# Attention over pairs of heads: scores, turned probabilities and values follow 1, 3 and 1 pieces of product behind each other in place of 3, 3 and 2

## The chip, the cores and the metric

The kernel runs on one NeuronCore of a Trainium2 chip. The metric is the device time of one execution in microseconds (us); of three executions of the kernel before, the median is 2475.26 us (2474.47 to 2476.66). Engines are named as in the profile: PE is the matrix engine (PEld its weight loads), DVE the vector engine, ACT the scalar engine, POOL the GpSimd engine, SP the engine whose queue issues the weight transfers.

## The reference, cut to what matters

The program is a two-layer decoder trunk over 256 rows of width 2048: a retention layer with its MLP, then a latent-attention layer with its MLP. The change touches only the attention of the second layer, with 16 heads, 128 + 64 query columns a head, 128 value columns a head:

```python
c_q = rms_norm(h @ w_dq, q_norm)
q = (c_q @ w_uq).reshape(b, s, H, MLA_NOPE_DIM + MLA_ROPE_DIM)
q_nope = rms_norm(q[..., :MLA_NOPE_DIM], q_nope_norm)
q_pe = apply_rope(rms_norm(q[..., MLA_NOPE_DIM:], q_pe_norm), cos[:, :, None], sin[:, :, None])
...
    sc = jnp.einsum('bhqd,bkhd->bhqk', qn, k_nope) + jnp.einsum('bhqr,bkr->bhqk', qp, k_pe)
    sc = sc.astype(jnp.float32) * scale
    sc = jnp.where(kpos[None, :] <= qpos[:, None], sc, -jnp.inf)
    p = jax.nn.softmax(sc, axis=-1).astype(v.dtype)
    return jnp.einsum('bhqk,bkhd->bqhd', p, v)
...
return o @ w_o
```

## The kernel before

Everything large is a product of weights with activations held on chip. Weights come in chunks ("pieces"): one SP transfer, then for each of two halves an ACT cast to a high part `wh` and a DVE subtraction to a low part `wl` (`split`, L185 and L186; pools of 5 each), then matmuls high x high, high x low, low x high (L246 to L248). A piece of the query product `uq` is 24 matmuls of 384 columns, one of the output product `wo` is 24 matmuls of 512 columns. In the attention stage the pieces are `uq0.0` to `uq7.2` (eight pairs of heads, three pieces a pair), then `wo`: pieces 0, 1, 2 of column block 0, the same of block 1, then the last piece of block 0 and of block 1, then blocks 2 and 3.

The order of all work beside the pieces is written out by a small queue. `later(n, fn)` files `fn` for `n` pieces from now; every piece ends with `tick()`, which raises the count of pieces by one and runs all that is due, in order of due number; `need(items, n)` runs the queue ahead of its due numbers, first due first, until a list has `n` entries. What a function of the queue emits stands in the source order of each engine at that point. The tile framework hands out buffers, sets the semaphores, and can place a ready instruction ahead of an earlier one that isn't ready, so the order of an engine in a trace differs in places from that of the source.

A pair of heads `b` passes through five functions:

- `query(b)`, run at the end of the pair's third piece: ACT scales the product into `qs` and squares it into `qu` (L981, L983), DVE sums (L984, L985) and makes `qn_m` (L174), POOL raises it to -1/2 (`qn_r`, L175), DVE multiplies `qs` by it (L992), rotates the last 64 columns (L850 to L853) and splits them into `qpp` (L1001, L1002). In the prediction this DVE work from L992 to L1002 is called the rotation.
- its `turn`: PE turns `qs` and `qpp` (`qntp`, `qptp`, L205), ACT copies them out of PSUM into `qt` (L1008) and `qpe` (L1013) and casts `qt` to its high part (L185), DVE makes the low part of `qt` (L186).
- `score(b)`: 20 matmuls into `s` (L1028 to L1033), which read both parts of `qt` and `qpe`; DVE masks into `p` (L1038) and takes the maximum `mx` (L1043); ACT the exponential (L1048); DVE the reciprocal (L1049); ACT the scaling (L1054).
- its `turn`: PE turns `p` into two PSUM tiles `ptp` (L1061), ACT copies each to `pt` (L1063).
- `values(b)`: PE multiplies into `ao` (L1072, L1073), ACT and DVE split it into `ot` (L185, L186), which is appended to `o_act`.

`qntp`, `qptp`, `ptp` and `ao` share two PSUM banks (tag `tp`). `qs`, `qu`, `qpp`, `qt`, `qpe`, `p` and `pt` share a pool of 14 buffers (`f2k`). A piece `g` of `wo` calls `need(o_act, 2g + 2)`, so the third piece wants six pairs done and the last pieces all eight.

With pieces counted from the start of `uq`, the due numbers before are: `query(b)` at 3b+3, its turn at 3b+6, `score` at 3b+9, the turn of `p` at 3b+12, `values` at 3b+14. At count 24 `wo` begins; at count 26 it needs six entries and `values(5)`, due at 29, is run ahead together with turn 7, score 6 and the turn of p 5; at count 30 it needs eight, and `values(6)`, the turn of p 7 and `values(7)` are run ahead one behind another. `x_tiles` also files four loads of residual blocks (`x_wo`, POOL's queue, L140) in this stretch.

Of the kernel before, what the change touches and what calls it, by code (L numbers as in the profile page):

```python
# [68 lines left out]
def yoco(ctx: ExitStack, tc: tile.TileContext, a):  # L69
# [4 lines left out]
    def f2k(shape, name, dtype=F32):  # L74
        return pool.tile([P, *shape], dtype, tag="f2k", bufs=14, name=name)

    def small(w, name):
        return pool.tile([P, w], F32, tag="small", bufs=36, name=name)
# [5 lines left out]
    def bank(tag, shape, name):  # L84
        t = psum.tile([P, 512], F32, tag=tag, bufs=4 if tag == "acc" else 2, name=name)
        return shaped(t, shape)

    def two_banks(name):
        return psum.tile([P, 2, 512], F32, tag="at", bufs=1, name=name)

    def act_tile(name, dtype=F32R):

        return pool.tile([P, 2, 2, S], dtype, tag="act", bufs=24, name=name)
# [5 lines left out]
    def later(n, fn):  # L99
        queue.append((clock[0] + n, next(count), fn))  # L100
# [67 lines left out]
    def rstds(total, sizes, name):  # L168

        w = total.free_size()  # L170
        m, r = small(w, f"{name}_m"), small(w, f"{name}_r")
        view = m.rearrange("p (t i h) -> p t i h", t=NT, i=len(sizes))
        for i, n in enumerate(sizes):
            nc.vector.tensor_scalar(view[:, :, i], total[:, :, i], 1.0 / n, EPS, op0=ALU.mult, op1=ALU.add)  # L174
        nc.gpsimd.tensor_tensor(r, m, neg_half[:, :w], op=ALU.pow)  # L175
        return r.rearrange("p (t i h) -> p t i h", t=NT, i=len(sizes))
# [5 lines left out]
    def split(h, l, src, scale=None):  # L182

        if scale is None:
            nc.scalar.copy(h, src)  # L185
            nc.vector.tensor_tensor(l, src, h.bitcast(F32), op=ALU.subtract)  # L186
        else:
            nc.scalar.activation(h, src, AF.Copy, scale=scale)
            nc.vector.scalar_tensor_tensor(
                l, src, scale, h.bitcast(F32), op0=ALU.mult, op1=ALU.subtract  # L190
            )
# [8 lines left out]
    def transposed(srcs, name):  # L200

        tp = bank("tp", [2, S], name)
        for j in range(2):
            for t in range(NT):
                nc.tensor.transpose(tp[:, j, t * P : (t + 1) * P], srcs(t, j), ident)  # L205
        return tp
# [637 lines left out]
    def pe_rope(dst, u, src, t, i, heads):  # L844


        def tab(j, lo, n):
            return pe_tabs[t][i][:, j, lo : lo + n].unsqueeze(1).to_broadcast([P, heads, n])

        nc.vector.tensor_tensor(dst, src, tab(0, 0, 64), op=ALU.mult)  # L850
        nc.vector.tensor_tensor(u[:, :, 0:32], src[:, :, 32:64], tab(1, 0, 32), op=ALU.mult)
        nc.vector.tensor_tensor(u[:, :, 32:64], src[:, :, 0:32], tab(1, 32, 32), op=ALU.mult)
        nc.vector.tensor_tensor(dst, dst, u, op=ALU.add)  # L853
# [122 lines left out]
    def query(acc, b):  # L976
        qr, qu = [], []
        sq = small(4 * NT, f"sq{b}").rearrange("p (t i h) -> p t i h", t=NT, i=2)
        for t in range(NT):
            q = f2k([2, 192], f"qs{b}{t}")  # L980
            nc.scalar.activation(q.rearrange("p h c -> p (h c)"), acc[t], AF.Copy, scale=rq[t])  # L981
            u = f2k([2, 192], f"qu{b}{t}")
            nc.scalar.activation(u.rearrange("p h c -> p (h c)"), acc[t], AF.Square, scale=rq[t])  # L983
            nc.vector.reduce_sum(sq[:, t, 0], u[:, :, 0:NOPE], axis=AX.X)  # L984
            nc.vector.reduce_sum(sq[:, t, 1], u[:, :, NOPE:], axis=AX.X)  # L985
            qu.append((q, u))
        r = rstds(sq, [NOPE, ROPE], f"qn{b}")
        for t in range(NT):
            q, u = qu[t]
            for i, cols in enumerate((slice(0, NOPE), slice(NOPE, NOPE + ROPE))):  # L990
                n = cols.stop - cols.start
                nc.vector.tensor_tensor(  # L992
                    q[:, :, cols], q[:, :, cols], r[:, t, i].unsqueeze(2).to_broadcast([P, 2, n]), op=ALU.mult
                )
            flat = u.rearrange("p h c -> p (h c)")
            pe = flat[:, 0 : 2 * ROPE]
            tmp = flat[:, 2 * ROPE : 4 * ROPE].rearrange("p (h c) -> p h c", h=2)
            pe_rope(pe.rearrange("p (h c) -> p h c", h=2), tmp, q[:, :, NOPE:], t, 1, 2)
            parts = f2k([2, 2, ROPE], f"qpp{b}{t}", F32R)
            pe = pe.rearrange("p (h c) -> p h c", h=2)  # L1000
            nc.vector.tensor_copy(parts[:, :, 0], pe)  # L1001
            nc.vector.tensor_tensor(parts[:, :, 1], pe, parts[:, :, 0].bitcast(F32), op=ALU.subtract)  # L1002
            qr.append((q, parts.bitcast(F32)))

        def turn():
            tp = transposed(lambda t, j: qr[t][0][:, j, 0:NOPE], f"qntp{b}")
            raw = f2k([2, S], f"qt{b}")
            nc.scalar.activation(raw, tp, AF.Copy, scale=gqn)  # L1008
            qt = [f2k([2, S], f"qt{b}{i}", F32R) for i in range(2)]
            split(qt[0], qt[1], raw)  # L1010
            tp = transposed(lambda t, j: qr[t][1][:, j].rearrange("p i c -> p (i c)"), f"qptp{b}")
            qpe = f2k([2, S], f"qpe{b}", F32R)
            nc.scalar.copy(qpe, tp)  # L1013
            later(3, lambda: score(b, qt, qpe))

        later(3, turn)

    def score(b, qt, qpe):

        sc = two_banks(f"s{b}")  # L1020
        for hh in range(2):
            for t in range(NT):
                dst = sc[:, hh, t * P : t * P + (t + 1) * P]
                qs = slice(t * P, (t + 1) * P)
                n = (t + 1) * P
                qh, ql = (i[:, hh, qs] for i in qt)
                kh, kl = (k_t[b][:, i, hh, :n] for i in range(2))
                nc.tensor.matmul(dst, qh, kh, start=True, stop=False)  # L1028
                nc.tensor.matmul(dst, qh, kl, start=False, stop=False)
                nc.tensor.matmul(dst, ql, kh, start=False, stop=False)  # L1030

                for i in range(2):
                    nc.tensor.matmul(dst, qpe[:, hh, qs], kpe_t[:, i, :n], start=False, stop=i == 1)  # L1033
        p = [f2k([2, (t + 1) * P], f"p{b}{t}") for t in range(NT)]
        for t in range(NT):
            cols = slice(t * P, t * P + (t + 1) * P)
            cut = mask[:, cols].unsqueeze(1).to_broadcast([P, 2, (t + 1) * P])
            nc.vector.tensor_tensor(p[t], sc[:, :, cols], cut, op=ALU.add)  # L1038
        neg = small(4, f"mx{b}")
        den = small(4, f"den{b}")  # L1040
        inv = small(4, f"inv{b}")
        for t in range(NT):
            nc.vector.tensor_reduce(neg[:, 2 * t : 2 * t + 2], p[t], axis=AX.X, op=ALU.max, negate=True)  # L1043
        for t in range(NT):
            for hh in range(2):
                i = 2 * t + hh
                view = p[t][:, hh]
                nc.scalar.activation(view, view, AF.Exp, bias=neg[:, i : i + 1], accum_out=den[:, i : i + 1])  # L1048
        nc.vector.reciprocal(inv, den)  # L1049
        for t in range(NT):  # L1050
            for hh in range(2):
                i = 2 * t + hh
                view = p[t][:, hh]
                nc.scalar.activation(view, view, AF.Copy, scale=inv[:, i : i + 1])  # L1054

        def turn():
            pt = []
            for hh in range(2):
                tp = bank("tp", [3 * P], f"ptp{b}{hh}")
                for i, src in enumerate((p[0][:, hh], p[1][:, hh, 0:P], p[1][:, hh, P:])):  # L1060
                    nc.tensor.transpose(tp[:, i * P : (i + 1) * P], src, ident)  # L1061
                o = f2k([3 * P], f"pt{b}{hh}")
                nc.scalar.copy(o, tp)  # L1063
                pt.append(o)
            later(2, lambda: values(b, pt))

        later(3, turn)

    def values(b, pt):
        o = bank("tp", [2, S], f"ao{b}")  # L1070
        for hh in range(2):
            nc.tensor.matmul(o[:, hh], v_s[b][:, 0, hh], pt[hh][:, 0:S], start=True, stop=False)  # L1072
            nc.tensor.matmul(o[:, hh, P:S], v_s[b][:, 1, hh], pt[hh][:, S:], start=False, stop=True)  # L1073
        v = act_tile(f"ot{b}")
        split_act(v, o)
        o_act.append(v)
# [109 lines left out]
```

## Time and profile before

| what | value |
|---|---|
| median of 3 runs | 2475.26 us |
| the profiled execution, its own time | 2474.51 us |
| its span | 2472.7 us |
| PE / PEld / DVE / ACT / POOL busy, share of the span | 99% / 83% / 88% / 65% / 10% |
| HBM traffic over the span | 210 GB/s |
| first and last turn of a query pair (`qntp` on PE) | 1578.2 us, 1697.1 us |
| first and last product of `ot` (`wo` on PE) | 1683.9 us, 1788.9 us |

The profile shows one execution; times in a trace are microseconds from the start of its span. A row of a timeline gives start, duration, engine, source line, operation, output and inputs by the program's names, and in brackets how long the engine had been idle and what released it. In the list of waits a row gives who waited for whom, the total, the number of waits and the longest. A window's row gives each engine's busy time in a stretch, the granted clock of PE (1.00 is full speed) and the DMA share. PE's matmuls are pipelined, so the start of the next one, not its own duration, tells what a matmul costs.

### The profile page before, as it was taken

How to read it: one execution, taken by the hardware profiler on the slowest of the kernel's cores; microseconds unless marked ns; L12 is line 12 of the kernel's file. 1: busy time of each engine (PE TensorE's matmuls, PEld its weight loads, DVE VectorE, ACT ScalarE, POOL GpSimd, SP SyncE). 2: the span in 40 equal slices, each digit the busy share in tenths (PEclk: the TensorE clock that was granted, in tenths of full speed). 3: DMA queues.
4: the chain of work that ended last, by engine and by line, in shares of the span. 5: the costliest groups of instructions: out<-in, count | busy, mean ns of one | idle time of the engine just before them, and what ended most of it. 6: DMA issues, size and time to landing. Idle time of an engine off the chain costs nothing.

```text
span 2472.7 us, 31711 instructions
## 1 busy us (share of the span) xinstructions
PE 2455.6 (99%) x11635; PEld 2060.0 (83%) x11635; DVE 2167.4 (88%) x2805; ACT 1606.1 (65%) x2253; POOL 251.6 (10%) x310
## 2 busy tenths in 40 slices
PE   9999999999999999999999999999999999999999
PEld 7888888888888888888888888998888888888887
DVE  7799899889899999999999967776689999999996
ACT  6566656556676667667666766676566666676663
POOL 7300011000010010110110101110000201101100
PEclk9999999999999999999999999999999999999999
DMA  9555567555564685684785564445545856857854
GB/s 328 211 174 205 196 205 234 199 192 201 198 236 182 209 262 216 213 254 172 246 263 196 192 228 168 153 155 179 199 174 199 261 212 209 268 203 225 266 192 153
DMA packets 93403, 521.04 MB, mean 211 GB/s; under 512 B 11072, under 2 KB 12224, under 8 KB 40000
## 3 DMA queue, kind: packets, MB, share of 16 engines
q1 hardware_dynamic: 71856, 472.83, 53.8%
q0 software_dynamic: 21248, 46.15, 8.5%
q8 instruction: 91, 1.49, 0.2%
q14 instruction: 64, 0.52, 0.1%
q10 hardware_dynamic: 144, 0.05, 0.0%
HBM read 479.14 MB, written 39.85 MB: 210 GB/s over the span
## 4 chain that ended last, share of the span: by engine, by line
PE 91%; DVE 4%; ACT 3%; issue 1%; POOL 1%; DMA 0%; SPq 0%; ACTq 0%; POOLq 0%; DVEq 0%
PE u_c L358 7%; PE u_c L356 7%; PE u_c L357 7%; PE d_c L357 6%; PE d_c L358 6%; PE d_c L356 6%; PE rk_acc L274 2%; PE rq_acc L274 2%; PE rp_c L356 2%; PE rp_c L357 2%; PE rp_c L358 2%; PE u_p L358 2%; PE u_p L356 2%; PE u_p L357 2%; PE d_p L356 2%; PE d_p L358 2%
## 5 line engine op out<-in xcount | busy, mean ns | idle before, releaser
L185 ACT CAST u_wh<-u_raw 128x1024 fp32r<-128x1024 f32 x362 | 347.9, 991 | 207.8 <-DVE u_raw L321 100.8
L185 ACT CAST d_wh<-d_raw 128x1024 fp32r<-128x1024 f32 x358 | 344.1, 993 | 202.5 <-DVE d_raw L321 93.9
L186 DVE TENSOR_TENSOR u_wl<-u_raw,u_wh 128x1024 fp32r<-128x1024 f32 x362 | 402.0, 1144 | 47.2 <-ACT u_wh L185 41.7
L186 DVE TENSOR_TENSOR d_wl<-d_raw,d_wh 128x1024 fp32r<-128x1024 f32 x358 | 397.8, 1146 | 40.1 <-ACT d_wh L185 35.5
L356 PE MATMUL u_c<-u_wh,n 128*128 128x512 f32 x706 | 276.4, 392 | 0.0
L357 PE MATMUL u_c<-u_wl,n 128*128 128x512 f32 x706 | 275.5, 390 | 0.0
L358 PE MATMUL u_c<-u_wh,n 128*128 128x512 f32 x706 | 274.9, 389 | 0.0
L356 PE MATMUL d_c<-d_wh,hid 128*128 128x512 f32 x654 | 256.0, 392 | 0.0
L357 PE MATMUL d_c<-d_wl,hid 128*128 128x512 f32 x654 | 255.4, 391 | 0.0
L358 PE MATMUL d_c<-d_wh,hid 128*128 128x512 f32 x654 | 254.6, 389 | 0.0
L185 ACT CAST rp_wh<-rp_raw 128x1024 fp32r<-128x1024 f32 (+1 forms) x166 | 160.7, 982 | 140.9 <-DVE rp_raw L321 64.9
L186 DVE TENSOR_TENSOR rp_wl<-rp_raw,rp_wh 128x1024 fp32r<-128x1024 f32 (+1 forms) x166 | 184.9, 1137 | 26.7 <-ACT rp_wh L185 24.4
L358 PEld LDWEIGHTS u_c<-u_wh,n 128*128 128x128 f32 x706 | 132.6, 188 | 27.4
L356 PEld LDWEIGHTS u_c<-u_wh,n 128*128 128x128 f32 x706 | 132.6, 188 | 26.9
L357 PEld LDWEIGHTS u_c<-u_wl,n 128*128 128x128 f32 x706 | 132.6, 188 | 26.7
L358 PEld LDWEIGHTS d_c<-d_wh,hid 128*128 128x128 f32 x654 | 122.8, 188 | 25.4
L356 PEld LDWEIGHTS d_c<-d_wh,hid 128*128 128x128 f32 x654 | 122.8, 188 | 25.2
L357 PEld LDWEIGHTS d_c<-d_wl,hid 128*128 128x128 f32 x654 | 122.9, 188 | 24.7
L150 POOL DMA_DIRECT2D xh<-d_c x48 | 41.6, 867 | 856.6 <-ACT d_c L373 854.7
L185 ACT CAST ro_wh<-ro_raw 128x1024 fp32r<-128x1024 f32 x88 | 85.7, 997 | 59.7 <-DVE ro_raw L321 25.7
L356 PE MATMUL rp_c<-rp_wh,a 128*128 128x512 f32 x286 | 111.9, 391 | 0.0
L357 PE MATMUL rp_c<-rp_wl,a 128*128 128x512 f32 x286 | 111.4, 390 | 0.2 <-DVE rp_wl L186 0.2
(465 smaller groups left out, 6075.6 us busy)
## 6 DMA issues: line engine op xcount, KB each, us to landing
u_raw<-in_mlp_w SPq DMA_DIRECT2D x128, 1024.0 KB, 5.2
d_raw<-in_mlp_w SPq DMA_DIRECT2D x120, 1024.0 KB, 4.9
rp_raw<-in_ret_w_gv SPq DMA_DIRECT2D x56, 1024.0 KB, 4.9
ro_raw<-in_ret_w_out SPq DMA_DIRECT2D x32, 1024.0 KB, 4.9
uq_raw<-in_mla_w_uq SPq DMA_DIRECT2D x24, 768.0 KB, 4.1
rq_raw<-in_ret_w_qk SPq DMA_DIRECT2D x16, 1024.0 KB, 5.0
rk_raw<-in_ret_w_qk SPq DMA_DIRECT2D x16, 1024.0 KB, 4.8
wo_raw<-in_mla_w_o SPq DMA_DIRECT2D x16, 1024.0 KB, 4.8
```

The costliest lines, as they stand in the source:

```text
L150: nc.gpsimd.dma_start(x_home[t][2 * p + j], part, accum_op=ALU.add)
L185: nc.scalar.copy(h, src)
L186: nc.vector.tensor_tensor(l, src, h.bitcast(F32), op=ALU.subtract)
L274: nc.tensor.matmul(acc[f], wh[:, cols], a.rearrange("p i s -> p (i s)"), start=k == 0, stop=k == nk - 1)
L356: nc.tensor.matmul(dst, ah, bh, start=n == 0, stop=False)
L357: nc.tensor.matmul(dst, ah, bl, start=False, stop=False)
L358: nc.tensor.matmul(dst, al, bh, start=False, stop=n == total[key] - 1)
```

## The change

Four numbers change. A pair's score follows its turned queries by one piece, not three; the turn of its probabilities follows the score by three pieces as before, by two for the last pair; the values follow that by one piece, not two. The turn of the last pair's queries follows `query` by two pieces, not three.

```diff
             nc.scalar.copy(qpe, tp)
-            later(3, lambda: score(b, qt, qpe))
-
-        later(3, turn)
+            later(1, lambda: score(b, qt, qpe))
+
+        later(3 if b < 7 else 2, turn)
...
                 pt.append(o)
-            later(2, lambda: values(b, pt))
-
-        later(3, turn)
+            later(1, lambda: values(b, pt))
+
+        later(3 if b < 7 else 2, turn)
```

By the same counting, the due numbers become: `query(b)` at 3b+3 and its turn at 3b+6 as before, `score` at 3b+7, the turn of `p` at 3b+10, `values` at 3b+11; for pair 7 the turn at 26, score at 27, the turn of `p` at 29, values at 30. Six entries of `o_act` are there at count 26 and eight at count 30, so `need` runs nothing ahead. No instruction is added or removed.

Between two turns of the steady stretch the source order on PE is, for a pair m and its predecessors:

| | before | after |
|---|---|---|
| at count 3k | turn of q (m), score (m-1), turn of p (m-2) | turn of q (m) |
| piece | `uq` 24 matmuls | `uq` 24 matmuls |
| at 3k+1 | | turn of p (m-1), score (m) |
| piece | `uq` 24 matmuls | `uq` 24 matmuls |
| at 3k+2 | values (m-2) | values (m-1) |
| piece | `uq` 24 matmuls | `uq` 24 matmuls |

`query(m+1)` stands at count 3k too, ahead of the turn of pair m, in both.

## The prediction

> **What bounds the kernel now.** I read the page first, then busy time by windows of the attention stage, then the list of waits there, last the timeline of one pair's turn, engine by engine. The page:
>
> ```profile
> span 2472.7 us, 31711 instructions
> PE 2455.6 (99%) x11635; PEld 2060.0 (83%) x11635; DVE 2167.4 (88%) x2805; ACT 1606.1 (65%) x2253; POOL 251.6 (10%) x310
> PE 91%; DVE 4%; ACT 3%; issue 1%; POOL 1%; DMA 0%; SPq 0%; ACTq 0%; POOLq 0%; DVEq 0%
> ```
>
> PE is busy 99% of the span and is 91% of the chain that ended last. No matmul is added or taken out, so the change can only move PE's idle time. How much of that lies in the stage it touches, by windows (first the length, then busy PE, PEld, DVE, ACT, POOL, the granted clock, the DMA share, GB/s):
>
> ```profile
> 1578.00:1625.00 47.00, 47.00 (x297) 46.50 (x296) 34.94 (x96) 31.79 (x64) 6.87 (x3) 1.00 0.43 150
> 1625.00:1628.00 3.00, 1.12 (x9) 0.85 (x8) 1.98 (x3) 3.00 (x6) 0.00 (x0) 1.00 0.68 215
> 1628.00:1680.00 52.00, 52.00 (x335) 51.43 (x334) 39.72 (x104) 37.26 (x83) 8.01 (x5) 1.00 0.47 158
> 1680.00:1700.00 20.00, 18.72 (x111) 16.16 (x110) 15.95 (x38) 15.10 (x31) 4.86 (x7) 1.00 0.70 236
> 1700.00:1740.00 40.00, 39.65 (x207) 33.72 (x207) 20.16 (x26) 22.64 (x48) 0.55 (x1) 1.00 0.41 138
> ```
>
> PE idles 1.88 us at 1625, 1.28 us at 1680 to 1700 and 0.35 us after that: 3.5 us in all, 0.14% of the time. That caps the gain. The waits of the stretch from 1550 to 1800, PE's own and three that matter below:
>
> ```profile
> PE qptp L205 <- DVE ot L186: 1.9, 1, 1.9
> PE qptp L205 <- ACT qt L1008: 1.2, 1, 1.2
> PE wo_acc L246 <- ACT ot L185: 0.3, 1, 0.3
> DVE qs L992 <- POOL qn_r L175: 12.5, 8, 1.8
> ACT p L1048 <- DVE mx L1043: 9.6, 7, 2.3
> ACT L1048 <- DVE mx L1043: 2.9, 1, 2.9
> ```
>
> Two of PE's waits are for one of the two shared PSUM banks (`qptp` until `ot` or `qt` has been read out), the third is the rush before the last piece of `wo`. The lower three show a second thing: the DVE runs late. It stands idle for POOL's `qn_r` at each of eight queries, and ACT's exponential then waits for `mx`, in all eight pairs.
>
> **The change part by part.**
>
> *What it removes.* All 3.5 us hang on crowding. Before, the turn of pair m, score m-1 and the turn of p m-2 stand together at one count, and at counts 26 and 30 `need` runs four and three functions behind one another. After, these lie a piece apart and nothing is run ahead. I take 3.0 us of the 3.5 as gone and bound the part by 0 and 3.5. (The 1.9 us wait comes one piece behind values, a distance that stays, so not all is certain.)
>
> *What it adds.* `score(m)` now stands one piece behind the turn of pair m, and reads the low part of `qt`. One turn as the trace has it, PE, ACT, POOL and DVE:
>
> ```profile
> 1644.97 0.60 PE L205 MATMUL qntp<-cst,qs 128*128 128x128 f32 x4
> 1645.76 0.30 PE L1028 MATMUL s<-kt,qt 128*128 128x128 f32 x1
> 1648.14 0.34 PE L246 MATMUL uq_acc<-uq_wh,cq 128*128 128x384 f32 x1
> 1650.58 0.49 PE L1061 MATMUL ptp<-cst,p 128*128 128x128 f32 x3
> 1652.68 0.49 PE L1061 MATMUL ptp<-cst,p 128*128 128x128 f32 x3
> 1652.92 0.42 PE L246 MATMUL uq_acc<-uq_wh,cq 128*128 128x384 f32 x1
> 1657.17 0.38 PE L1072 MATMUL ao<-pt,v 128*128 128x256 f32 x1
> 1647.24 0.71 ACT L1008 ACTIVATE qt<-qntp,gqn 128x512 f32<-128x512 f32 x1
> 1650.43 0.84 ACT L185 CAST uq_wh<-uq_raw 128x768 fp32r<-128x768 f32 x1 [2.47 <-PE uq_acc L248]
> 1651.17 0.61 ACT L185 CAST qt<-qt 128x512 fp32r<-128x512 f32 x1
> 1651.69 0.58 ACT L1013 CAST qpe<-qptp 128x512 fp32r<-128x512 f32 x1
> 1647.58 2.31 POOL L175 TENSOR_TENSOR qn_r<-qn_m,neg_half 128x8 f32<-128x8 f32 x1 [15.24 <-DVE qn_m L174]
> 1649.92 0.96 DVE L992 TENSOR_TENSOR qs<-qs,qn_r 128x256 f32<-128x256 f32 x3 [1.53 <-POOL qn_r L175]
> 1653.26 0.29 DVE L1002 TENSOR_TENSOR qpp<-qu,qpp 128x128 fp32r<-128x128 f32 x1
> 1653.47 0.95 DVE L186 TENSOR_TENSOR uq_wl<-uq_raw,uq_wh 128x768 fp32r<-128x768 f32 x1
> 1654.34 0.68 DVE L186 TENSOR_TENSOR qt<-qt,qt 128x512 fp32r<-128x512 f32 x1
> 1653.62 0.86 ACT L1063 COPY pt<-ptp 128x384 f32<-128x384 f32 x2
> 1656.38 0.40 ACT L1048 ACTIVATE p<-p,mx 128x128 f32<-128x128 f32 x1 [1.91 <-DVE mx L1043]
> ```
>
> Call the start of the turn T (1644.97). The turn takes PE 0.8 us (to 1645.76), a score 2.4 us (1645.76 to 1648.14), a piece 4.25 us (1652.92 to 1657.17), the two `ptp` 0.5 us. The low part of `qt` is done at 1655.02, T + 10.05. ACT's high part is not what holds it: the cast of `qt` ends at 1651.78. DVE makes the low part only behind the rotation of the query that was run at the same count (1649.92 to 1653.55), which waited for POOL's `qn_r` until T + 4.95. None of these engines' places is touched by the change: `query(m+1)` still stands ahead of turn m. The low part of `qt` should therefore still end near T + 10. Before, its reader came a whole pair later, behind the next turn; after, it comes at T + 0.8 + 4.25 + 0.5 = T + 5.5 by the source.
>
> What is queued behind the waiting score on PE is everything: the rest of `uq`, values, the next turn. So a wait there is lost time, unless matmuls of the next piece are set ahead of the score. The trace shows that the tile framework's planner does this: the two `ptp` stand 2.4 and 4.5 us into a piece (1650.58 and 1652.68 against 1648.14) which the source puts behind them. Filled that way with the whole next piece, PE reaches the score at T + 9.8. So the wait for each pair lies between 0.25 us (10.05 less 9.8) and 4.5 us (10.05 less 5.5). Where in between? The order is fixed before the run, from when the planner believes an input to be ready; its error for this DVE chain can be read off ACT, which stands at the exponential behind the same rotation for 1.91 us here, 12.5 us (9.6 and 2.9) in eight pairs, 1.6 us each. The first turn, which had no score beside it, is the closest likeness to the new order:
>
> ```profile
> 1578.24 0.60 PE L205 MATMUL qntp<-cst,qs 128*128 128x128 f32 x4
> 1586.30 0.68 ACT L1008 ACTIVATE qt<-qntp,gqn 128x512 f32<-128x512 f32 x1
> 1589.04 0.69 DVE L186 TENSOR_TENSOR qt<-qt,qt 128x512 fp32r<-128x512 f32 x1
> ```
>
> There the low part ends at T + 11.5, 1.7 us behind T + 9.8. I take 1.8 us a pair, between these, for the seven pairs 0 to 6 whose turn has a query beside it: 12.6 us (bounds 1.8 and 31.5).
>
> *Pair 7.* Its turn at count 26 has no query beside it, and score 7 comes a `wo` piece later, which with 512 columns for 384 is no shorter than the 4.25 us. In the trace its low part of `qt` ended at 1700.50, 3.7 us from the start of its turn (rows below), before 0.8 + 4.25. Covered, at nothing; with that cover gone it would cost one wait of 3.7 less 0.8, 2.9 us.
>
> ```profile
> 1696.80 0.60 PE L205 MATMUL qntp<-cst,qs 128*128 128x128 f32 x4
> 1699.82 0.68 DVE L186 TENSOR_TENSOR qt<-qt,qt 128x512 fp32r<-128x512 f32 x1
> L140 POOL DMA_DIRECT2D x_wo<-xh x8: 536/538/627, 1667.5 to 1687.9; - x8
> L463 DVE TENSOR_TENSOR x_wo<-wo_acc,x_wo x8: 680/682/687, 1737.2 to 1789.5; 128x512 f32<-128x512 f32 x8
> ```
>
> *Values one piece behind the turned p, not two.* `pt` is two ACT copies, 0.86 us together; the score (2.4 us) and a piece (4.25 us) lie between. Nothing, covered. *The loads of `x_wo`* on POOL's queue: one is no longer run ahead and comes two pieces later; the last was issued at 1687.9, its first reader came at 1737.2, 49 us later. Nothing.
>
> **Sum.** -3.0 + 12.6 = +9.6 us on the profiled execution's own 2474.51 us (span 2472.7 and 1.8 around it): 2484.1 us. The median of the runs stands 0.75 us higher, so I put 2484.5 us against it.
>
> A rule that speaks against the change: the Trainium skill, "TensorE: Matmul & The Clock Gate", section "What's actually happening", says that PE falls to half its clock once it has idled through a window of about 3.4 us. The 1.88 us idle at 1625 came with a granted clock of 1.00, so up to there trace and rule agree. By the rule waits of 1.8 us cost only themselves; the 4.5 us waits of rival C would cost more than their own length, by an amount no row here shows.
>
> **The rivals.**
>
> A, *the low part of `qt` goes ahead of the rotation on DVE*. DVE idles 1.53 us before 1649.92, waiting for POOL; with the score no longer between turn and piece, ACT's cast of `uq_wh` (released by PE at 1650.43, 2.4 us earlier without the score) and so its cast of `qt` would end near T + 4.4. If DVE then has the low part in the queue ahead of the rotation, it ends by T + 5.2, and the score at T + 5.5 waits for nothing. It decides at that one place. For it: the pool of 14 buffers is less crowded, as `qt`, `qpe` and `pt` live shorter. Against: in all seven such turns of the trace the low part stands behind the rotation, the first turn included, where no score was in the way. Time: 2475.26 - 3.5 to 2475.26, 2471.8 to 2475.3.
>
> The Trainium skill, "Perfetto Trace Analysis", section "Identifying Performance Opportunities", holds that repeated gaps on the engine that should be saturated can mean too few buffers for the next tile. By that rule the two waits for PSUM banks would go and the result would be A; the trace agrees on their cause, and says that they are worth 3.1 us.
>
> B, *the change doesn't do what it says*: the score is set behind the whole next piece and more, as late as the low part is, so the distances in the source hardly matter on PE. For it: the second `ptp` slid by a whole piece. Against: the planner is 1.6 us off at this chain. Time: 2475.26 - 3.0 + 7 x 0.25 = 2474.
>
> C, *the score keeps its place in the source*: 7 x 4.5 = 31.5, less 3.0: 2504 us. For it: before, each score stood right behind its turn. Against: there its inputs were ready.
>
> **How the numbers follow.** Forecast (waits of 0.9 to 3.4 us a pair, 2478 to 2496 us) 0.55; A 0.25; B 0.10; C 0.10. The range is 2471.5 to 2496: it takes in A and B, and leaves out C (0.10), the forecast's upper tail (0.04) and a gain above PE's idle time (0.05). The forecast's own range is 2478 to 2496. A measurement of this kernel can tell about 0.2% (5 us) from no change: faster than 2470.3 needs more than the 3.5 us that the windows show, 0.06; within, A and B nearly whole and the forecast's lowest edge, 0.32; slower, 0.62.
>
> **What would show it.** Right: in each of seven pairs a wait of PE at L1030 of the score, released by DVE `qt` L186, 1 to 3 us; the low part behind L1002 and 9 to 12 us after `qntp`; PE idle of some 13 us between 1578 and 1690; `qptp` waits and the rush at the last `wo` piece gone; the stage from the first `qntp` to the last `wo` matmul longer by 8 to 12 us, all else the same. Wrong: `qt` L186 ahead of L992 on DVE and no idle PE (A); the score behind a whole further piece (B); a granted clock under 1.00. A difference outside this stage would make the whole prediction wrong.

## The result, and the profile after

The changed kernel takes 2488.26 us (median of 6 runs, 2487.09 to 2489.23) against 2476.45 us for the one before in the same comparison: a ratio of 1.0047, 95% interval 1.0037 to 1.0058. It is slower by 11.8 us; 9.2 us over the earlier median were forecast.

The page of the changed kernel:

```profile
span 2485.3 us, 31705 instructions
PE 2461.8 (99%) x11635; PEld 2061.4 (83%) x11635; DVE 2166.0 (87%) x2805; ACT 1606.3 (65%) x2253; POOL 250.8 (10%) x310
PE 90%; DVE 4%; ACT 3%; issue 1%; POOL 1%; DMA 0%; SPq 0%; ACTq 0%; POOLq 0%
```

The counts of PE, DVE, ACT and POOL work are those of before; the span is 12.6 us longer. Of these, 1.4 us had arisen before the first turn of a query (1579.67 against 1578.24), more than half of it in the first 20 matmuls of the program, which the change doesn't touch; at the last `wo` matmul the kernel was 12.6 us behind, and it stayed so to the end. So the stage itself lost 11.2 us. Its windows in the changed kernel (same columns as before):

```profile
1579.70:1632.00 52.30, 48.82 (x305) 47.01 (x304) 36.38 (x99) 34.76 (x69) 6.85 (x3) 1.00 0.40 139
1632.10:1635.50 3.40, 3.40 (x17) 3.22 (x16) 0.88 (x2) 0.00 (x0) 0.00 (x0) 0.50 0.87 337
1635.50:1697.00 61.50, 57.03 (x358) 54.13 (x358) 42.48 (x109) 40.68 (x90) 8.99 (x7) 1.00 0.42 156
1697.00:1760.00 63.00, 60.95 (x310) 51.04 (x311) 36.13 (x63) 39.82 (x81) 5.98 (x9) 1.00 0.48 161
```

PE now idles 3.48, 4.47 and 2.05 us in the three long windows, 10.0 us where it was 3.5. The second row is new: 3.4 us at a granted clock of 0.50, worth 1.7 us. Idle time (+6.5) and the clock (+1.7) make 8.2 of the 11.2 us; the remaining 3 us lie in time that the profile counts as busy. Counted from the start of one matmul to the start of the next, against the usual step of each kind in the kernel before, the steps that end in a wait lose 7.5 us more than before and those at half clock 1.6; the last 2.1 us are spread over the other steps, under 0.2 us each, and were not traced to a cause. What PE waited for, in the list of waits of this stage:

```profile
PEld s L1030 <- DVE qt L186: 10.6, 6, 2.0
PE s L1030 <- DVE qt L186: 9.0, 6, 1.7
DVE qs L992 <- POOL qn_r L175: 12.5, 8, 1.8
PEld qptp L205 <- DVE ot L186: 0.6, 3, 0.2
PE wo_acc L246 <- ACT ot L185: 0.4, 1, 0.4
```

The wait that the forecast named heads PE's list: the score's third matmul, the first that reads the low part of `qt`, in six pairs: 9.0 us of idle time, 10.1 us counted from start to start. PE's two waits for a PSUM bank, 3.1 us before, are gone from the matmuls' list. One turn of the steady stretch, PE, ACT, POOL, DVE:

```profile
1637.14 0.60 PE L205 MATMUL qntp<-cst,qs 128*128 128x128 f32 x4
1649.18 0.49 PE L1061 MATMUL ptp<-cst,p 128*128 128x128 f32 x3
1650.38 0.23 PE L1028 MATMUL s<-kt,qt 128*128 128x128 f32 x1
1650.78 0.49 PE L1061 MATMUL ptp<-cst,p 128*128 128x128 f32 x3
1652.64 0.33 PE L1030 MATMUL s<-kt,qt 128*128 128x128 f32 x1 [1.37 <-DVE qt L186]
1638.71 0.57 ACT L981 ACTIVATE qs<-uq_acc,cq_r 128x384 f32<-128x384 f32 x1
1646.68 0.84 ACT L185 CAST uq_wh<-uq_raw 128x768 fp32r<-128x768 f32 x1 [1.24 <-PE uq_acc L248]
1647.42 0.68 ACT L1008 ACTIVATE qt<-qntp,gqn 128x512 f32<-128x512 f32 x1
1649.50 0.61 ACT L185 CAST qt<-qt 128x512 fp32r<-128x512 f32 x1
1642.98 2.31 POOL L175 TENSOR_TENSOR qn_r<-qn_m,neg_half 128x8 f32<-128x8 f32 x1 [19.17 <-DVE qn_m L174]
1645.33 0.96 DVE L992 TENSOR_TENSOR qs<-qs,qn_r 128x256 f32<-128x256 f32 x3 [1.53 <-POOL qn_r L175]
1650.84 0.28 DVE L1002 TENSOR_TENSOR qpp<-qu,qpp 128x128 fp32r<-128x128 f32 x1
1651.04 0.95 DVE L186 TENSOR_TENSOR uq_wl<-uq_raw,uq_wh 128x768 fp32r<-128x768 f32 x1
1651.91 0.68 DVE L186 TENSOR_TENSOR qt<-qt,qt 128x512 fp32r<-128x512 f32 x1
```

The high part of `qt` is done at 1650.11 (1649.50 + 0.61). DVE starts the low part only at 1651.91, behind the rotation of the next query and four low parts of weights set among it (the last at 1651.04), and ahead of the rotation DVE had stood idle for 1.53 us of POOL's 2.31 us instruction. PE, at `ptp` by 1650.78, waits. But the places differ from the forecast: measured from the start of the turn, the low part ends at 15.4 us, not 10, and the score stands not one piece behind its turn but at 13.2 us (1650.38), with nearly all three pieces of the next pair set ahead of it.

### The profile page after: what moved, and what is told of

It is laid out like the page before. It is cut to its first block, busy times and chain, and to the rows that moved or that the text cites. A ratio compares the mean times of both kernels' runs of the same rounds, so it can differ in the third digit from the quotient of the medians.

```text
span 2485.3 us, 31705 instructions
## 1 busy us (share of the span) xinstructions
PE 2461.8 (99%) x11635; PEld 2061.4 (83%) x11635; DVE 2166.0 (87%) x2805; ACT 1606.3 (65%) x2253; POOL 250.8 (10%) x310
## 4 chain that ended last, share of the span: by engine, by line
PE 90%; DVE 4%; ACT 3%; issue 1%; POOL 1%; DMA 0%; SPq 0%; ACTq 0%; POOLq 0%
PE u_c L357 7%; PE u_c L358 7%; PE u_c L356 7%; PE d_c L358 6%; PE d_c L357 6%; PE d_c L356 6%; PE rk_acc L274 2%; PE rq_acc L274 2%; PE rp_c L356 2%; PE rp_c L357 2%; PE rp_c L358 2%; PE u_p L358 2%; PE u_p L356 2%; PE u_p L357 2%; PE d_p L356 2%; PE d_p L358 2%
## 5 line engine op out<-in xcount | busy, mean ns | idle before, releaser
L358 PEld LDWEIGHTS d_c<-d_wh,hid 128*128 128x128 f32 x654 | 122.8, 188 | 25.4
```

Of the source, the lines that this page charges most:

```text
L358: nc.tensor.matmul(dst, al, bh, start=False, stop=n == total[key] - 1)
```

## The experiments

Theory 1: PE's loss is the planner's error on one chain (POOL's power, then on DVE the rotation and the low part of `qt`). The score is set where the planner believes that part to be ready, and waits for the rest. No trace shows what the planner believes; it is inferred from the order that it made. Rivals: the other three numbers; ACT, which makes the high part late behind casts of weights; the distance in the source itself. Each ratio is to the kernel before on the same chip, with its 95% interval.

| kernel | median us, before | ratio | PE at L1030 |
|---|---|---|---|
| score_three | 2474.20, 2476.53 | 0.9993 (0.9984 to 1.0001) | none |
| turn_first | 2482.58, 2476.53 | 1.0027 (1.0016 to 1.0038) | none |
| no_pow | 2474.50, 2476.53 | 0.9993 (0.9984 to 1.0002) | none |
| low_on_pool | 2505.09, 2476.53 | 1.0117 (1.0103 to 1.0131) | 18.3 us in 7 |
| score_two | 2485.76, 2475.80 | 1.0039 (1.0027 to 1.0052) | 8.7 us in 6 |
| pow_twice | 2504.27, 2475.80 | 1.0113 (1.0097 to 1.0128) | 13.8 us in 6 |
| score_one_alone | 2487.11, 2475.80 | 1.0045 (1.0032 to 1.0057) | 6.4 us in 5 |
| score_three_b | 2474.13, 2475.80 | 0.9992 (0.9983 to 1.0001) | none |

**score_three**: the first number put back for pairs 0 to 6. With the other numbers as they are, the values of pair 7 come ahead of those of pair 6, so that these two enter the output product in each other's place; the work is the same.

```diff
-            later(1, lambda: score(b, qt, qpe))
+            later(3 if b < 7 else 1, lambda: score(b, qt, qpe))
```

> The score of pairs 0 to 6 goes back to three pieces behind its turned queries; all else as after. Theory 1 (PE waits at L1030 for the low part of qt, which DVE makes 1.5 to 2 us later than the planner believed, because it stands there behind the next query's rotation and that waits for POOL): the low part is long done, no wait at L1030, the granted clock stays at 1.00 throughout the stage, 2473 to 2478 us, at or a little under before. Theory 2 (the loss comes from the other three numbers, from values one piece closer and the last pair's): it stays near 2486 to 2489 us.

2474.2 us, no wait at L1030, granted clock 1.00 throughout the profiled execution. The whole loss hangs on the score's place; theory 2 of the expectation is out.

**turn_first**: the turn of pair m emitted ahead of query m+1.

```diff
-        gemm(a["mla_w_uq"], b * 3, cq, 12, Q_NB, f"uq{b}", lambda acc, b=b: query(acc, b))
+        gemm(a["mla_w_uq"], b * 3, cq, 12, Q_NB, f"uq{b}", lambda acc, b=b: later(0, lambda: query(acc, b)))
```

> At each count the turn of pair m is emitted ahead of query m+1 instead of behind it; the four numbers as after. Theory 1: DVE makes the low part of qt ahead of the rotation, within some 6 us of the turn's start in place of 11.5 to 15.6 us; the waits at L1030 (9.0 us on PE in six pairs) go, and with them the half-clock stretch: 2472 to 2477 us. Rival (ACT makes the high part late because casts of weights stand ahead of it, wherever the query stands): waits at L1030 stay, 2485 to 2489 us. A second risk: the query's reading of its product comes later and PE waits for an accumulator; then waits at L246 of uq show up instead.

The low part ends 3.0 to 5.8 us after the turn's start in pairs 0 to 6, and no score waits. The time is a miss all the same, 6 us over before. PE's list and two windows of this kernel:

```profile
PE qptp L205 <- DVE ot L186: 4.7, 4, 2.5
PE ao L1072 <- ACT qt L1008: 3.3, 1, 3.3
```

```profile
1616.50:1619.90 3.40, 3.40 (x12) 3.40 (x11) 2.18 (x6) 3.40 (x7) 0.00 (x0) 0.50 0.66 234
1708.60:1715.50 6.90, 6.16 (x17) 5.03 (x18) 2.52 (x3) 3.22 (x6) 0.00 (x0) 0.51 0.44 152
```

The wait has moved: now the turn's second half waits for a bank that `ot` still holds, and the clock falls twice. (The profiled execution is one of two with a mean granted clock of 0.997; the other five list 0.999.) So the place behind the query explains the wait at L1030, and the rival on ACT falls: ACT's high part was done 2.3 to 5.0 us after the turn's start in pairs 0 to 6. But read out there, `ot` and `qt` free the shared banks too late.

**no_pow**: the link that the planner is thought to misjudge is taken out, nothing is moved in the source.

```diff
-        nc.gpsimd.tensor_tensor(r, m, neg_half[:, :w], op=ALU.pow)
+        (nc.vector.tensor_scalar(r, m, 1.0, None, op0=ALU.mult) if len(sizes) == 2 else nc.gpsimd.tensor_tensor(r, m, neg_half[:, :w], op=ALU.pow))
```

> The power of -1/2 over a query's sums is left out: DVE copies the mean square in place of POOL's 2.3 us instruction, so the queries are scaled wrongly. Order of the rest as after. Theory 1: the rotation starts some 2 us earlier and the low part behind it is no longer later than the planner believed: waits at L1030 fall from 9.0 us to under 2, time 2474 to 2480 us. Rival (ACT's late high part): nothing changes at L1030, 2485 to 2489 us.

2474.5 us. Its timeline for the same pair:

```profile
1631.01 0.60 PE L205 MATMUL qntp<-cst,qs 128*128 128x128 f32 x4
1645.41 0.30 PE L1030 MATMUL s<-kt,qt 128*128 128x128 f32 x1
1637.18 0.16 DVE L175 TENSOR_SCALAR qn_r<-qn_m 128x8 f32<-128x8 f32 x1
1638.12 0.95 DVE L992 TENSOR_TENSOR qs<-qs,qn_r 128x256 f32<-128x256 f32 x3
1644.60 0.69 DVE L186 TENSOR_TENSOR qt<-qt,qt 128x512 fp32r<-128x512 f32 x1 [0.28 <-ACT qt L185]
```

The low part still ends late, 14.3 us after the turn's start, and the score's third matmul stands at 14.4 us: nearly the places of the changed kernel. But DVE is now ready before ACT (0.28 us idle), and PE doesn't wait. So a late low part isn't what costs; one that is later than planned is. One caution: the planner answered the edit, and in pairs 1 to 6 it set the score 3 to 10 matmuls further on. Pair 0 is free of that: the same 60 matmuls lead from the turn's first matmul to the score's third, the low part ends 10.1 us after the turn's start in place of 11.5, and the wait is 0.07 us in place of 1.40.

**low_on_pool**: the low part of `qt` made by POOL.

```diff
-            split(qt[0], qt[1], raw)
+            nc.scalar.copy(qt[0], raw); nc.gpsimd.tensor_tensor(qt[1], raw, qt[0].bitcast(F32), op=ALU.subtract)
```

> The low part of qt is made by POOL instead of DVE, so it no longer stands behind the rotation and the weights' low parts on DVE; all else as after. Theory 1: the waits at L1030 shrink by what DVE's queue added, from 1.5 to 2 us a pair to under 1, unless POOL itself takes longer than 2 us for it or has a query's power ahead of it; 2476 to 2484 us. Rival (ACT's late high part): waits as they are or longer by POOL's slower instruction, 2487 us or more.

A miss, through a cost mis-sized: the subtraction that DVE does in 0.68 us takes POOL 3.32 us on average, 1.3 us in pairs 0 and 7 and 3.4 to 5.5 us in the others. The wait list's row and the group's:

```profile
PE s L1030 <- POOL qt L1010: 18.3, 7, 4.4
```

```profile
L1010 POOL TENSOR_TENSOR qt<-qt,qt 128x512 fp32r<-128x512 f32 x8 | 26.6, 3321 | 44.0 <-ACT qt L1010 33.7 <-issue 10.3
```

It tells nothing of DVE's queue, since the new instruction is longer than what it avoids; it does show what a longer POOL instruction in this chain costs PE. Of the time lost, some 10 us are not waits but the clock, at half for 20.5 us in the profiled execution.

**score_two**: the score alone one piece further on.

```diff
-            later(1, lambda: score(b, qt, qpe))
+            later(2 if b < 7 else 1, lambda: score(b, qt, qpe))
...
-        later(3 if b < 7 else 2, turn)
+        later(2, turn)
```

> Of pairs 0 to 6 the score alone is moved one piece on: two pieces behind the turned queries, and the turn of p two behind the score, so that p and the values stay where they are after the change. Theory 1 (the planner sets the score where it believes the low part of qt to be ready, some 12 to 13.5 us after the turn's start, which is already beyond two pieces; what PE waits is the planner's error on the chain POOL, rotation, low part): waits at L1030 stay at 1.3 to 2 us a pair, 2483 to 2489 us. Rival (PE waits for as long as the source's place is ahead of the low part, so 4.25 us more distance is enough): waits gone, 2474 to 2478 us.

```profile
PE s L1030 <- DVE qt L186: 8.7, 6, 1.7
```

2485.8 us, and that wait is the 9.0 us of the changed kernel almost unchanged; in pairs 0 to 6 the score's third matmul stands within 0.05 us of where it stood, counted from the turn. A piece more in the source bought nothing, since the planner had already set it further on: the rival on distance is out.

**pow_twice**: the suspected link doubled.

```diff
-        nc.gpsimd.tensor_tensor(r, m, neg_half[:, :w], op=ALU.pow)
+        (nc.gpsimd.tensor_tensor(small(w, f"{name}_x"), m, neg_half[:, :w], op=ALU.pow) if len(sizes) == 2 else None, nc.gpsimd.tensor_tensor(r, m, neg_half[:, :w], op=ALU.pow))
```

> POOL raises a query's sums to -1/2 twice, the first time into a buffer nobody reads: 2.3 us more ahead of the rotation, all else as after. Theory 1: each of the six waits at L1030 grows by 1.5 to 2.3 us, together from 9 to 18 to 23 us, with more stretches at half the clock: 2496 to 2510 us. Rival (the waits don't hang on POOL): 2486 to 2490 us.

```profile
DVE qs L992 <- POOL qn_r L175: 25.4, 8, 3.5
PE s L1030 <- DVE qt L186: 13.8, 6, 3.4
PE uq_acc L247 <- DVE uq_wl L186: 7.0, 5, 2.0
```

DVE's wait for POOL doubles (12.5 to 25.4 us). PE's waits at L1030 grow to 13.8 us, less than expected, and waits for weights' low parts, which stand in the same DVE queue, grow from 0.5 to 7.0 us: 20.8 us together, and 2504 us. The rest of the time lost goes with the clock, at half for 27.3 us in the profiled execution, the slowest of the four (2507.8 us). The trace also holds the best evidence for theory 1: from the first turn to the last product of values PE's 909 matmuls stand in exactly the order of the changed kernel. The second power left no mark in the planner's order, and PE waited for it.

**score_one_alone**: the kernel before with the first number alone.

```diff
-            later(3, lambda: score(b, qt, qpe))
+            later(1, lambda: score(b, qt, qpe))
...
-        later(3, turn)
+        later(5, turn)
```

(the second line is that of the turn of `p`, set so that `p` and the values keep the places that they have before)

> The kernel before with one number changed: score one piece behind the turned queries, and the turn of p five behind the score, so that p and the values keep the places that they have before. Theory 1: the waits at L1030 come back with this one number, six or seven of 1.3 to 2.3 us: 2483 to 2491 us. Rival (it takes the crowding of values and turns a piece apart as well): 2474 to 2478 us.

```profile
PE s L1030 <- DVE qt L186: 6.4, 5, 1.7
```

2487.1 us: the loss comes with this one number. Two stretches at half clock stand beside it (1591 and 1690 us). In pairs 2 to 5 the planner chose other places, the score's third matmul 4.1 to 5.7 us after the turn's start in place of 14.6 to 15.7, and the waits are of the same size, 1.0 to 1.7 us.

**score_three_b**: as score_three, with the last pairs in order.

```diff
-            later(1, lambda: score(b, qt, qpe))
+            later(3 if b < 7 else 1, lambda: score(b, qt, qpe))
...
-        later(3 if b < 7 else 2, turn)
+        later(3 if b < 6 else 2, turn)
```

(again that of the turn of `p`)

> The score three pieces behind as before, values one piece behind as after, the turn of p three behind and two for pairs 6 and 7, so that the pairs enter the output product in their order. Theory 1: no wait at L1030, the waits for a PSUM bank that before had mostly gone: 2473 to 2477 us, at most 3 us under before. Rival (what the closer values bring is lost at the runs ahead of the queue, which stay at count 26): the same as before, within 1 us.

```profile
1579.00:1640.00 61.00, 59.53 (x376) 58.08 (x376) 46.07 (x128) 40.66 (x79) 9.19 (x4) 1.00 0.42 147
1640.00:1700.00 60.00, 60.00 (x371) 56.66 (x370) 45.54 (x110) 45.16 (x100) 10.54 (x11) 1.00 0.55 194
1700.00:1740.00 40.00, 40.00 (x209) 33.93 (x209) 21.42 (x28) 23.98 (x50) 0.61 (x2) 1.00 0.43 143
```

PE idles 1.5 us in the stage in place of 3.5, and the median is 1.7 us under before; the interval reaches 1.0001, so a gain is likely but not settled. Some of it may be the clock: four of the fifteen executions of the kernel before list a mean granted clock under 1.00, and none of the eleven here. It beats the changed kernel clearly.

## Why the prediction was right

*What bounds.* Right: only PE's idle time could move, and 3.5 us was the most to win. The medians of score_three, no_pow and score_three_b lie 1.7 to 2.3 us under before, with intervals that reach 1.0001 or 1.0002.

*What it removes.* Forecast 3.0 of 3.5 us. The bank waits of 3.1 us went, and the time of these three kernels shows about 2 us of that, a gain not clear of no change. The third wait, the rush ahead of `wo`, stayed (0.3 us before, 0.4 after).

*What it adds.* The mechanism was the one named, and no_pow and pow_twice show it by taking its cause away and doubling it. The size was taken too high: 1.8 us for each of seven pairs, 12.6 us, came out as six waits of 1.2 to 1.7 us on PE, 9.0 us in the list and 10.1 from start to start. Pair 1 has none: there its low part ended 0.5 us ahead of the matmul. What filled the gap to the measured total was not in the sum: 1.7 us of half clock, 2.1 us spread over PE's steps, and in the profiled executions 1.4 us from ahead of the stage. That the sum came within 2.6 us of the measured difference is partly luck.

*Where it stands.* Here a step failed: "The low part of `qt` should therefore still end near T + 10" and, with it, the bounds T + 5.5 and T + 9.8 for the score. I had taken the places on ACT and DVE as untouched. Only pair 0 kept them (11.5 us, a step of 1.79 us into its third score matmul, as read from the first turn of before). In the others ACT reads out the turned `qs` at 10.2 to 10.5 us where it had been 2.3 in the steady turn. In the turn shown it does so behind five casts of weights, and starts the next query later (1638.71, 1.6 us after the turn's start, where it had begun before it): the exponentials of the delayed score now stand just ahead of it. The planner set far more than one piece ahead of the score, so it seems to have known of most of this. The sum still held because the wait was sized from ACT's lateness at `mx` and from pair 0, that is from the planner's error, and this hardly depended on the place: pair 0 at 11.5 us, pairs 2 to 6 at 14.6 to 15.7 and score_one_alone at 4.1 to 5.7 wait alike. The bounds of 0.25 and 4.5 us a pair hung on places that the score didn't have, and bounded nothing.

*Rivals.* A (low part ahead of the rotation) did not come; turn_first forced it from the source, and forced like that it didn't pay. B was half right: the score slid behind more than a piece, but the wait stayed. C did not come.

*The clock.* The sum let waits of 1.8 us cost only themselves. In the changed kernel a wait of 1.66 us was followed by 3.4 us at a granted clock of 0.50 (from 1632.1), worth 1.7 us more. The forecast had gone by the Trainium skill, "TensorE: Matmul & The Clock Gate", section "What's actually happening", by which the clock falls after an idle window of about 3.4 us. The trace disagrees if that means a window without work; the length of the stretch, 3.4 us, agrees.

*Its own signs.* Of those named for being right, the waits at L1030 came in six pairs of seven, the `qptp` waits went, and the stage grew by 11.2 us, inside 8 to 12. The low part at 9 to 12 us came in pair 0 alone (13.5 to 15.6 in pairs 1 to 6), and the idle time of PE was 10.0 us in the whole stage, not 13. One sign named for being wrong came too, a granted clock under 1.00, and 1.4 us arose outside the stage.

*Pair 7, values, loads of `x_wo`.* Covered, as forecast: no wait on PE for any of them above 0.4 us.

## What to carry to other kernels

Where a planner fixes the order, the distance between a producer and its reader in the source is not the slack. The slack is what the planner leaves between them, less its error, and that error shows where an engine waits again and again for a chain through one instruction. Before moving a reader closer, look which engine already waits for its producers: here such a wait cost nothing on ACT (12.5 us in eight pairs, before) and was paid in full on PE. Two runs together separate "late" from "later than planned": one that takes the suspected link out, and one that doubles it, each with a look at whether the planner changed the order.

## What the hardware showed that was not expected

The granted clock of PE fell to 0.50 in stretches of 3.41 us, or twice that, behind waits mostly shorter than such a stretch. In the attention stage of the profiled executions this came once in the changed kernel and in score_two, for two such lengths in score_one_alone, three in turn_first, six in low_on_pool and eight in pow_twice; not in the kernel before, score_three, score_three_b or no_pow. The profiled execution of the kernel before doesn't speak for all: on the chip of the first four experiments 13 of its 23 executions list a mean granted clock of 0.999 or 0.998. These took 2476.4 to 2478.3 us, the other ten 2474.5 to 2476.4.

Which waits do it can be read off the traces in good part. In each, the stretches begin a whole number of steps of 3.413 us after the clock's first rise, so the time falls into fixed windows. Two windows of the kernel before, which share its idle time of 1.88 us, and two of the changed kernel:

```profile
1623.07:1626.48 3.41, 2.69 (x17) 2.41 (x16) 1.60 (x3) 3.41 (x9) 0.00 (x0) 1.00 0.24 40
1626.48:1629.89 3.41, 2.25 (x20) 2.25 (x21) 3.26 (x10) 3.41 (x7) 0.00 (x0) 1.00 0.61 229
```

```profile
1587.75:1591.16 3.41, 2.03 (x12) 1.54 (x10) 3.38 (x8) 3.36 (x6) 0.00 (x0) 1.00 0.58 216
1628.71:1632.13 3.42, 1.76 (x14) 1.48 (x13) 3.27 (x5) 0.90 (x3) 0.00 (x0) 1.00 0.95 323
```

Only the last, with PE busy for 1.76 us, is followed by half clock. Over the ten traces the clock fell behind every window in which PE was busy for less than 1.65 us (13 windows, some at the end of the program), behind 6 of the 14 with 1.70 to 2.05 us, and behind none with more. So what counts here is how much of one window is idle, and where a wait lies against the windows; no run tested this by moving a wait.

On POOL a 128x512 float32 subtraction took 1.3 to 5.5 us, 3.32 on average, where DVE takes 0.68. A power over 128x8 took 2.2 us on average; a second one right behind it took 1.6. (The profile calls its spans on POOL rough.)
